# First norm without its gain and bias on the rows, idle transposes at the start, last norm by halves, in a one-core encoder layer

## The chip, the cores and the metric

The kernel runs on one core of a Trainium2 chip. The metric is the time of the whole program on the device in microseconds (us); lower is better. The engines are TensorE (PE; its weight loads are listed apart as PEld), VectorE (DVE), ScalarE (ACT), GpSimd (POOL) and SyncE (SP), which issues most of the DMAs.

## The reference

One post-norm encoder layer over 512 tokens of width 1024, in float32. The parts that the change touches are the first layer norm, the norm after the attention (its input), and the last norm.

```python
def layer_norm(x, g, b):
    xf = x.astype(jnp.float32)
    mu = jnp.mean(xf, axis=-1, keepdims=True)
    var = jnp.mean(jnp.square(xf - mu), axis=-1, keepdims=True)
    y = (xf - mu) * lax.rsqrt(var + LN_EPS)
    return (y * g.astype(jnp.float32) + b.astype(jnp.float32)).astype(x.dtype)
...
    h = layer_norm(x, emb_ln_g, emb_ln_b)
    for i in range(DEPTH):
        z = h @ w_in[i]
        ...
        mix = jnp.concatenate([a_na, a_mla], axis=-1) @ w_o[i]
        h = layer_norm(DN_ALPHA * h + mix, ln1_g[i], ln1_b[i])
        ffn = peer_ffn(h, peer_w_q[i], peer_sub_keys[i], peer_u[i], peer_v[i])
        gate = jax.nn.sigmoid(h @ ple_gate_w[i] + ple_gate_b[i])
        ple = gate * (p[i] @ ple_w[i])
        h = layer_norm(DN_ALPHA * h + ffn + ple, ln2_g[i], ln2_b[i])
    return h
```

`a_na` is a neighbourhood attention, `a_mla` a latent attention, and `peer_ffn` looks up 128 of 16384 experts for each token.

## The kernel before

The 512 tokens are four chunks of 128 rows. `h[0]` to `h[3]` hold the rows of the residual, one token on each partition, 1024 values along it. The matmuls need the transposed activations, `hTh` and `hTl`: every float32 operand is kept as a rounded part (`...h`, "high") and the rest (`...l`, "low"), and a product is three matmuls (`mm3`, lines 93 to 95). `split` (lines 78 and 79) makes the two parts: ScalarE rounds, then VectorE subtracts. So each piece of weight passes through ScalarE and VectorE before PE can use it. A weight is loaded into a buffer `raw`, of which there are three; a fourth load waits until the first has been split.

The first stage (lines 242 to 261) goes over the chunks. For each chunk `layer_norm` takes mean and variance with `bn_stats` and `bn_aggr`, a square root on ScalarE, a reciprocal and a refinement step on VectorE (four operations on one column each), and then two passes over the rows: subtract the mean and multiply by the gain (line 131), multiply by the reciprocal deviation and add the bias (line 134). Gain and bias lie in `eg` and `eb`, broadcast over all partitions by a DMA each (`row_bcast`, line 138). `transpose_to` turns the rows in eight PE transposes in two groups of four, each group into one PSUM tile, and splits each group. Then 24 matmuls against a 1024 x 512 piece of `w_in`, held as `aTh` and `aTl`, make the chunk's values, which ScalarE copies to `v_na` (line 261). The piece of `w_in` comes in four quarters of 256 rows, loaded and split after the first chunk's transposes (lines 252 to 256).

The attention heads follow (lines 287 to 556), first the eight heads of the neighbourhood attention, then those of the latent attention, each as 32 units of scores, softmax and product; the order on PE is written out by hand there, scores two units ahead. Then `w_o` is applied, the residual `h` times `ALPHA` is added (lines 572 and 585), and `layer_norm` is called with `ln1`'s gain and bias (`lg`, `lb`) and with row sums that the addition has gathered; in this form it takes the variance from a squaring pass on ScalarE (line 121). Routing, the expert stage and the last norm (lines 1013 to 1024) come after. In the expert stage the order of VectorE is written by hand; chunk 0 is fed by gathered expert rows, and chunks 1 to 3 by matmuls into the PSUM tiles `acc`. The last norm adds `acc` to the rows in two halves with their sums, calls `layer_norm` and stores each chunk with one DMA.

Where no order is written by hand, a planner at build time makes the order of every engine and queue: it goes through the program with its own estimates of times, and gives an engine that is free the earliest instruction in program order that is ready. The order is then fixed, and on the chip each engine executes it in turn. The memory of a pool that opens later is that of pools closed before; a load into it waits for their last readers.

Of the kernel before, what the change touches and what calls it, by code (L numbers as in the profile page):

```python
# [18 lines left out]
D = 1024  # L19
# [26 lines left out]
FEED_NA = 2.75  # L46
FEED_LAT = 1.0
# [7 lines left out]
def tile_encoder_layer(ctx: ExitStack, tc: tile.TileContext, A: dict, out: bass.AP):  # L55
# [48 lines left out]
    def layer_norm(r, g, b, sums=None, scr=None):  # L104

        ve = small.tile([128, 1], F32, name="ln_ve")
        mu = small.tile([128, 2], F32, name="ln_mu")
        if sums is None:
            st = small.tile([128, 2, 6], F32, name="ln_st")
            for i in range(2):  # L110
                nc.vector.bn_stats(st[:, i, :], r[:, i * 512:(i + 1) * 512])
            nc.vector.bn_aggr(mu, st)
            nc.vector.tensor_scalar(ve, mu[:, 1:2], EPS, None, op0=OP.add)
            neg = None
        else:
            neg = mu[:, 1:2]
            nc.vector.tensor_tensor(neg, sums[:, 0:1], sums[:, 1:2], op=OP.add)
            nc.vector.tensor_scalar(neg, neg, -1.0 / D, None, op0=OP.mult)
            sq = wst.tile([128, D], F32, name="raw", bufs=3) if scr is None else scr
            ss = small.tile([128, 1], F32, name="ln_ss")  # L120
            nc.scalar.activation(sq, r, AF.Square, bias=neg, accum_out=ss)
            nc.vector.tensor_scalar(ve, ss, 1.0 / D, EPS, op0=OP.mult, op1=OP.add)
# [7 lines left out]
        if neg is None:  # L130
            nc.vector.scalar_tensor_tensor(r, r, mu[:, 0:1], g, op0=OP.subtract, op1=OP.mult)
        else:
            nc.vector.scalar_tensor_tensor(r, r, neg, g, op0=OP.add, op1=OP.mult)
# [17 lines left out]
    def ps_tile(name, bufs=2):  # L151
        return ps6.tile([128, 512], F32, name=name, bufs=bufs)
# [17 lines left out]
    def transpose_to(dst_h, dst_l, src, c):  # L170

        for g in range(2):
            ps = ps_tile("tr")
            for i in range(4):
                d = 4 * g + i
                nc.tensor.transpose(ps[:, i * 128:(i + 1) * 128], src[:, d * 128:(d + 1) * 128], ident)
            v = ps.rearrange("p (a b) -> p a b", b=128)
# [64 lines left out]
    with tc.tile_pool(name="ln0", bufs=1) as ln0:  # L242
        nc.sync.dma_start(h[0], A["x"][0:128, :])
        eg = row_bcast(ln0, A["emb_ln_g"], "eg")
        eb = row_bcast(ln0, A["emb_ln_b"], "eb")
        for c in range(1, 4):
            nc.sync.dma_start(h[c], A["x"][c * 128:(c + 1) * 128, :])
# [864 lines left out]
```

## Time and profile before

| | us |
|---|---|
| three timed runs | 1636.96, 1638.03, 1643.42 |
| median | 1638.03 |
| the profiled execution | 1644.48 |
| its span on the core | 1642.7 |

The profile is of one execution. Its page gives busy time by engine, the chain of work that ended last, and the costliest groups of instructions. The timeline lists single instructions: start, duration, engine, line, operation, output and inputs, and in brackets how long the engine had been idle before it and what ended that. "x3" after a row means that neighbouring rows are merged, and then the duration is that from the first start to the last end. A table by stage gives the busy time of the engines in stretches of the span. Durations of neighbouring instructions on an engine overlap by some hundredths to tenths of a us, so that the step from one start to the next is shorter than the duration.

### The profile page before, as it was taken

What the parts mean: (1) busy time and instruction counts of PE and PEld (TensorE: products, weight loads), DVE (VectorE), ACT (ScalarE), POOL (GpSimd) and SP (SyncE); (2) the same over time, 40 slices, a digit from 0 to 9 for tenths busy, and PEclk for the clock granted to TensorE, in tenths of its full rate; (3) what the DMA queues carried; (4) which work ended last, traced back from release to release, by engine and by line L of the source; (5) the groups of instructions that cost most, each with busy time, mean ns of one, the idle gap of its engine ahead of it and who ended that gap; (6) DMA issues with size and microseconds to landing.
All of it is one profiled execution on the core that took longest, in us unless ns stands there. A gap on an engine that the chain in (4) does not pass through costs nothing.

```text
span 1642.7 us, 23609 instructions
## 1 busy us (share of the span) xinstructions
PE 1564.1 (95%) x8195; PEld 1309.7 (80%) x8195; DVE 1328.0 (81%) x2959; ACT 671.3 (41%) x1190; POOL 553.3 (34%) x407
## 2 busy tenths in 40 slices
PE   6999899999999999996899999999999999999997
PEld 4788677888777767784788888888898888888885
DVE  7366794699999999995778888878888888877776
ACT  3356684433324626682333333333343333333343
POOL 1013100000114453200455555555455565543200
PEclk9999999999999999998899999999999999999999
DMA  7242340332469988756899999999999999987763
GB/s 223 61 127 75 86 124 14 119 90 78 118 219 318 373 320 301 288 226 233 309 340 323 359 325 350 361 323 336 354 324 334 358 327 350 344 291 257 260 237 110
DMA packets 190583, 409.13 MB, mean 249 GB/s; under 512 B 14592, under 2 KB 100992, under 8 KB 187392
## 3 DMA queue, kind: packets, MB, share of 16 engines
q1 hardware_dynamic: 141696, 234.06, 41.9%
q0 software_dynamic: 48768, 173.56, 29.3%
q8 instruction: 65, 1.06, 0.3%
q14 instruction: 54, 0.44, 0.1%
HBM read 372.64 MB, written 31.98 MB: 246 GB/s over the span
## 4 chain that ended last, share of the span: by engine, by line
PE 40%; DMA 22%; issue 15%; DVE 14%; POOL 7%; ACT 2%; SPq 1%; DVEq 0%; POOLq 0%; ACTq 0%
DMA gat<-in_u_rows_dram,i_sel 11%; DMA gat<-in_v_rows_dram,i_sel 8%; PE hp L631 4%; PE acc L93 4%; PE acc L95 4%; PE acc L94 4%; POOL gat L925 3%; PE tr L804 3%; PE pj L93 3%; PE mm L93 3%; PE pj L94 3%; PE pj L95 3%; PE mm L94 3%; PE mm L95 3%; POOL gat L936 3%
## 5 line engine op out<-in xcount | busy, mean ns | idle before, releaser
L93 PE MATMUL acc<-v_hi,a_hi 128*128 128x512 f32 x756 | 297.6, 394 | 14.2 <-ACT a_hi L78 14.2
L95 PE MATMUL acc<-v_hi,a_lo 128*128 128x512 f32 x756 | 296.8, 393 | 0.0
L94 PE MATMUL acc<-v_lo,a_hi 128*128 128x512 f32 x756 | 294.9, 390 | 0.0
L925 POOL DMA_INDIRECT gat<-in_u_rows_dram,i_sel x128 | 203.2, 1588 | 260.2 <-DVE scr L927 147.8
L936 POOL DMA_INDIRECT gat<-in_v_rows_dram,i_sel x128 | 210.6, 1646 | 202.7 <-DVE base L938 172.6
L78 ACT CAST a_hi<-gt 128x384 fp32r<-128x384 f32 x126 | 64.9, 515 | 478.7 <-DVE gt L995 476.5
L95 PE MATMUL hp<-hTh,wlo 128*128 128x320 f32 x672 | 211.2, 314 | 17.9 <-DVE wlo L79 17.5
L93 PE MATMUL hp<-hTh,whi 128*128 128x320 f32 x672 | 208.7, 311 | 1.0 <-ACT ge L633 1.0
L94 PE MATMUL hp<-hTl,whi 128*128 128x320 f32 x672 | 208.2, 310 | 0.0
L631 PE MATMUL hp<-whole,raw 128*128 128x320 f32 x704 | 200.3, 433 | 0.0
L78 ACT CAST whi<-raw 128x1024 fp32r<-128x1024 f32 (+3 forms) x137 | 138.4, 1010 | 131.2 <-PE mm L94 53.1
L79 DVE TENSOR_TENSOR wlo<-raw,whi 128x1024 fp32r<-128x1024 f32 (+3 forms) x137 | 159.8, 1167 | 37.7 <-ACT whi L78 37.3
L79 DVE TENSOR_TENSOR v_lo<-v_raw,v_hi 128x1024 fp32r<-128x1024 f32 x126 | 153.7, 1220 | 39.4 <-DMA v_raw<-in_v_rows_dram 19.6
L927 DVE SCALAR_TENSOR_TENSOR scr<-gat,h 128x1024 f32<-128x1024 f32 x128 | 156.5, 1223 | 35.5 <-DMA gat<-in_u_rows_dram,i_sel 33.7
L938 DVE SCALAR_TENSOR_TENSOR base<-gat,hdot,base 128x1024 f32<-128x1024 f32 x128 | 164.1, 1282 | 21.6 <-DMA gat<-in_v_rows_dram,i_sel 20.1
L93 PEld LDWEIGHTS acc<-v_hi,a_hi 128*128 128x128 f32 x756 | 142.3, 188 | 41.9 <-ACT a_hi L78 15.4
L95 PEld LDWEIGHTS acc<-v_hi,a_lo 128*128 128x128 f32 x756 | 142.3, 188 | 33.7 <-DVE a_lo L79 1.4
L631 PEld LDWEIGHTS hp<-whole,raw 128*128 128x128 f32 x704 | 128.9, 190 | 45.6
L94 PEld LDWEIGHTS acc<-v_lo,a_hi 128*128 128x128 f32 x756 | 142.5, 188 | 27.6
L78 ACT CAST v_hi<-v_raw 128x1024 fp32r<-128x1024 f32 x126 | 131.9, 1047 | 54.6 <-PE acc L95 33.4
L95 PEld LDWEIGHTS hp<-hTh,wlo 128*128 128x128 f32 x672 | 127.3, 189 | 26.0 <-DVE wlo L79 25.9
L79 DVE TENSOR_TENSOR a_lo<-gt,a_hi 128x384 fp32r<-128x384 f32 x126 | 70.4, 559 | 80.4 <-ACT a_hi L78 79.1
(343 smaller groups left out, 2863.9 us busy)
## 6 DMA issues: line engine op xcount, KB each, us to landing
raw<-in_uT_dram SPq DMA_DIRECT2D x128, 512.0 KB
v_raw<-in_v_rows_dram SPq DMA_DIRECT2D x128, 512.0 KB
g_dram<-g_st SPq DMA_DIRECT2D x24, 1024.0 KB
gt<-g_dram SPq DMA_DIRECT2D x16, 1536.0 KB
raw<-in_w_in_dram SPq DMA_DIRECT2D x17, 512.0 KB
raw<-in_w_q_dram SPq DMA_DIRECT2D x16, 512.0 KB
na_b<-in_na_bias_dram POOLq DMA_DIRECT2D x32, 128.0 KB
raw<-in_w_o_dram SPq DMA_DIRECT2D x8, 512.0 KB
```

Of the source, the lines that this page charges most:

```text
L78: nc.scalar.copy(hi, src)
L79: nc.vector.tensor_tensor(lo, src, r32(hi), op=OP.subtract)
L93: nc.tensor.matmul(ps, a[0], b[0], start=start, stop=False)
L94: nc.tensor.matmul(ps, a[0], b[1], start=False, stop=False)
L95: nc.tensor.matmul(ps, a[1], b[0], start=False, stop=stop)
L631: nc.tensor.matmul(ps[:, :N_U], u[:, k], whole[:, k, :], start=(k == 0), stop=(k == 7))
L804: nc.tensor.matmul(ps[:, i * 128:(i + 1) * 128], oj[:, 4 * r + i, :], oi[:, 4 * r + i, :], start=True, stop=True)
L925: nc.gpsimd.indirect_dma_start(out=u[:], out_offset=None, in_=u_rows, in_offset=bass.IndirectOffsetOnAxis(ap=i_sel[:, c, k:k + 1], axis=0))
L927: nc.vector.scalar_tensor_tensor(scr, u, 1.0, h[c], op0=OP.mult, op1=OP.mult, accum_out=hdot[:, c, k:k + 1])
L936: nc.gpsimd.indirect_dma_start(out=u[:], out_offset=None, in_=v_rows, in_offset=bass.IndirectOffsetOnAxis(ap=i_sel[:, c, k:k + 1], axis=0))
L938: nc.vector.scalar_tensor_tensor(base[c], u, hdot[:, c, k:k + 1], base[c], op0=OP.mult, op1=OP.add)
```

## The change

The first norm's rows are now only centred and scaled, in one pass with two column operands. Gain and bias of this norm are loaded as columns, `e_gain` and `e_bias` (128 partitions x 8), each by a DMA of single floats, and are applied by ScalarE on the way out of the transposes, eight activations for each chunk into new tiles `tr_y`, which are then split as before. The rows in `h` lack them therefore; they are put in before the first use of the residual, after the heads: two row broadcasts into the buffers of `lg` and `lb`, and a multiplication and an addition for each chunk. `ln1`'s gain and bias are loaded into the same buffers afterwards.

The loads at the start are in another order: `x` of chunk 0, gain, bias, then quarters of the weight and chunks of `x` in turn; the fourth quarter, and `h[3]` behind it, come in the loop. 24 transposes of the identity matrix into a PSUM tile that nothing reads stand ahead of the first norm.

The last norm takes mean and variance with `bn_stats` for all chunks, adds `acc` without row sums, and does each of its two passes and the store in halves of 512 columns. `layer_norm` with sums stays for `ln1`.

```diff
+WARM = 24
...
-    def layer_norm(r, g, b, sums=None, scr=None):
...
+    def inv_dev(ve):
...
+    def row_stats(r):
+
+        st = small.tile([128, 2, 6], F32, name="ln_st")
+        for i in range(2):
+            nc.vector.bn_stats(st[:, i, :], r[:, i * 512:(i + 1) * 512])
+        mu = small.tile([128, 2], F32, name="ln_mu")
+        nc.vector.bn_aggr(mu, st)
+        ve = small.tile([128, 1], F32, name="ln_ve")
+        nc.vector.tensor_scalar(ve, mu[:, 1:2], EPS, None, op0=OP.add)
+        return mu[:, 0:1], inv_dev(ve)
+
+    def layer_norm(r, g, b, sums):
...
-    def transpose_to(dst_h, dst_l, src, c):
+    def transpose_to(dst_h, dst_l, src, c, affine=None):
...
+            if affine is not None:
+                gain, bias, pool = affine
+                y = pool.tile([128, 512], F32, name="tr_y", bufs=3)
+                for i in range(4):
+                    d = 4 * g + i
+                    nc.scalar.activation(y[:, i * 128:(i + 1) * 128], ps[:, i * 128:(i + 1) * 128], AF.Identity,
+                                         scale=gain[:, d:d + 1], bias=bias[:, d:d + 1])
+                ps = y
...
-        eg = row_bcast(ln0, A["emb_ln_g"], "eg")
-        eb = row_bcast(ln0, A["emb_ln_b"], "eb")
-        for c in range(1, 4):
-            nc.sync.dma_start(h[c], A["x"][c * 128:(c + 1) * 128, :])
+        gain = ln0.tile([128, 8], F32, name="e_gain")
+        bias = ln0.tile([128, 8], F32, name="e_bias")
+        for t, src in ((gain, A["emb_ln_g"]), (bias, A["emb_ln_b"])):
+            nc.sync.dma_start(t, bass.AP(tensor=src.tensor, offset=src.offset, ap=[[1, 128], [128, 8]]))
+        raws = []
+        for kk in range(3):
+            raws.append(wst.tile([128, 2, 512], F32, name="raw", bufs=3))
+            nc.sync.dma_start(raws[kk], A["w_in"][kk * 256:(kk + 1) * 256, 1024:1536].rearrange(
+                "(k p) n -> p k n", p=128))
+            if kk < 2:
+                nc.sync.dma_start(h[1 + kk], A["x"][(1 + kk) * 128:(2 + kk) * 128, :])
+        warm = ps_tile("mm")
+        for i in range(WARM):
+            nc.tensor.transpose(warm[:, 0:128], ident, ident)
         for c in range(4):
-            layer_norm(h[c], eg, eb)
-            transpose_to(hTh, hTl, h[c], c)
+            mu, y = row_stats(h[c])
+            nc.vector.tensor_scalar(h[c], h[c], mu, y, op0=OP.subtract, op1=OP.mult)
+            transpose_to(hTh, hTl, h[c], c, (gain, bias, ln0))
             if c == 0:
                 for kk in range(4):
-                    raw = wst.tile([128, 2, 512], F32, name="raw", bufs=3)
-                    nc.sync.dma_start(raw, A["w_in"][kk * 256:(kk + 1) * 256, 1024:1536].rearrange(
-                        "(k p) n -> p k n", p=128))
-                    split(aTh[:, 2 * kk:2 * kk + 2], aTl[:, 2 * kk:2 * kk + 2], raw)
+                    if kk == 3:
+                        raws.append(wst.tile([128, 2, 512], F32, name="raw", bufs=3))
+                        nc.sync.dma_start(raws[kk], A["w_in"][kk * 256:(kk + 1) * 256, 1024:1536].rearrange(
+                            "(k p) n -> p k n", p=128))
+                        nc.sync.dma_start(h[3], A["x"][384:512, :])
+                    split(aTh[:, 2 * kk:2 * kk + 2], aTl[:, 2 * kk:2 * kk + 2], raws[kk])
...
     lnp = p3.enter_context(tc.tile_pool(name="lnp", bufs=1))
+
+    eg = row_bcast(lnp, A["emb_ln_g"], "lg")
+    eb = row_bcast(lnp, A["emb_ln_b"], "lb")
+    for c in range(4):
+        nc.vector.tensor_tensor(h[c], h[c], eg, op=OP.mult)
+        nc.vector.tensor_tensor(h[c], h[c], eb, op=OP.add)
     lg = row_bcast(lnp, A["ln1_g"], "lg")
     lb = row_bcast(lnp, A["ln1_b"], "lb")
...
     for c in range(4):
-        fsum = None
+        r = base[c]
+        halves = [slice(hf * 512, (hf + 1) * 512) for hf in range(2)]
         if c >= NGC:
-            fsum = small.tile([128, 2], F32, name="fsum", bufs=2)
-            for hf in range(2):
-                hs = slice(hf * 512, (hf + 1) * 512)
-                nc.vector.scalar_tensor_tensor(base[c][:, hs], base[c][:, hs], 1.0, acc[c - NGC][hf], op0=OP.mult,
-                                               op1=OP.add, accum_out=fsum[:, hf:hf + 1])
-        layer_norm(base[c], lg, lb, fsum, scr)
-        nc.sync.dma_start(out[c * 128:(c + 1) * 128, :], base[c])
+            for hf, hs in enumerate(halves):
+                nc.vector.tensor_tensor(r[:, hs], r[:, hs], acc[c - NGC][hf], op=OP.add)
+        mu, y = row_stats(r)
+        for hs in halves:
+            nc.vector.scalar_tensor_tensor(r[:, hs], r[:, hs], mu, lg[:, hs], op0=OP.subtract, op1=OP.mult)
+            nc.vector.scalar_tensor_tensor(r[:, hs], r[:, hs], y, lb[:, hs], op0=OP.mult, op1=OP.add)
+            nc.sync.dma_start(out[c * 128:(c + 1) * 128, hs], r[:, hs])
```

`inv_dev` holds the square root, reciprocal and refinement that `layer_norm` had inline.

More of the change, by code (lines that the diff above doesn't have):

```diff
@@ L102, in rsqrt_refine @@
         nc.vector.tensor_tensor(y, t, y0, op=OP.mult)
-    def layer_norm(r, g, b, sums=None, scr=None):
[L106 to L122, printed above, removed]
+    def inv_dev(ve):
         sd = small.tile([128, 1], F32, name="ln_sd")
```

16 lines of the change are left out of this document (12 added, 4 removed).

## The prediction

> **What bounds the kernel now.** I read the page first (span, engines), then the table by stage, then the timelines of the first 47 us and of the last 20, because the change touches these two ends and one place between.
>
> ```profile
> span 1642.7 us, 23609 instructions
> PE 1564.1 (95%) x8195; PEld 1309.7 (80%) x8195; DVE 1328.0 (81%) x2959; ACT 671.3 (41%) x1190; POOL 553.3 (34%) x407
> 0.00:16.00 16.00, 2.38 (x9) 1.85 (x9) 10.50 (x25) 4.29 (x7) 0.71 (x6) 1.00 0.90 313
> 16.00:33.00 17.00, 15.60 (x65) 11.97 (x65) 16.39 (x33) 7.68 (x13) 0.52 (x1) 1.00 0.67 184
> ```
>
> (After the stretch and its length: busy time of PE, PEld, DVE, ACT, POOL, then granted clock, DMA share, GB/s.) TensorE (PE) is busy for 95% of the span; what it loses, it loses mostly at the ends. In the first 16 us it works 2.38 us, and in the next 17 VectorE (DVE) is busy for 16.39. The head is set by arriving data, then by VectorE:
>
> ```profile
> 4.09 1.29 DVE L111 BATCH_NORM_STATS2 ln_st<-h 128x6 f32<-128x512 f32 x2 [3.04 <-DMA h<-in_x_dram]
> 7.19 1.28 DVE L131 SCALAR_TENSOR_TENSOR h<-h,ln_mu,eg 128x1024 f32<-128x1024 f32 x1 [1.39 <-DMA eg<-in_emb_ln_g_dram]
> 10.78 1.94 PE L176 MATMUL tr<-ident,h 128*128 128x128 f32 x8 [10.78 <-DVE h L134]
> 17.42 0.38 SPq L254 DMA_DIRECT2D raw<-in_w_in_dram  x1
> 21.00 1.05 ACT L78 CAST aTh<-raw 128x1024 fp32r<-128x1024 f32 x1 [2.03 <-DMA raw<-in_w_in_dram]
> 23.09 1.22 DVE L79 TENSOR_TENSOR aTl<-raw,aTh 128x1024 fp32r<-128x1024 f32 x1
> 25.84 0.59 ACT L261 COPY v_na<-pj 128x512 f32<-128x512 f32 x1
> 31.29 0.40 PE L95 MATMUL pj<-aTh,hTl 128*128 128x512 f32 x1
> 32.86 0.50 PE L93 MATMUL pj<-aTh,hTh 128*128 128x512 f32 x1 [0.29 <-ACT hTh L78]
> 46.30 0.59 ACT L261 COPY v_na<-pj 128x512 f32<-128x512 f32 x1 [5.72 <-PE pj L95]
> ```
>
> The first norm waits 1.39 us for the broadcast gain; but what ends chunk 0 (its copy to `v_na` at 25.84) is the fourth quarter of the weight: issued at 17.42 when a `raw` buffer came free, cast at 21.00, split by VectorE only at 23.09. From its arrival to the copy it is 25.84 - 21.00 = 4.8 us. After that each chunk is PE's work plus a gap (31.29 + 0.23 to 32.86: 1.3 us) of transposes, cast and split. The fourth copy, at 46.30, is the end of the stage and the point by which I judge the head; PE is dense behind it.
>
> **The head, step by step.** Out go two 512 KB broadcasts and, on VectorE, two 1.28 us passes a chunk; one subtract-and-multiply pass comes in.
>
> ```profile
> L189 DVE TENSOR_SCALAR p_exp<-p_exp,rs 128x512 f32<-128x512 f32 x32 | 15.4, 482 | 0.5
> L189 DVE TENSOR_SCALAR p_exp<-p_exp,rs 128x256 f32<-128x256 f32 x32 | 11.7, 364 | 0.9
> DMA packets 313, 0.08 MB, mean 198 GB/s; under 512 B 256, under 2 KB 282, under 8 KB 313
> q1 hardware_dynamic: 313, 0.08, 88.7%
> 10.70:13.00 2.30, 1.94 (x8) 1.57 (x8) 2.30 (x5) 0.83 (x2) 0.00 (x0) 1.00 1.04 403
> ```
>
> 256 columns more cost 0.118 us, so 1024 cost 0.482 + 2 x 0.118 = 0.72, and VectorE is relieved of 4 x (2.56 - 0.72) = 7.4 us. The gain and bias now come as 2 x 1024 descriptors of 4 bytes. The two DMA rows are the stretch 20.2 to 20.6 us, in which `gq` and `gk` land (256 packets of 8 and 12 bytes): 0.4 us x 16 engines x 88.7% = 5.7 us for all 313, at most 22 ns a small one; less 57 larger ones, some 10. So 2048 take 1.3 to 2.8 us. At the 403 GB/s of the last row 512 KB take 1.3 us. First quarter of the weight: 4.1 (x there) + 1.3 to 2.8 + 1.3 = 6.7 to 8.2. Its cast and split (1.05 + 1.22, and 0 to 1 behind other VectorE work) free the buffer at 9 to 11.5; the fourth quarter needs 21.0 - 17.4 = 3.6 us from issue, and 4.8 to the copy: 17.4 to 19.9. I take 19.3, nearer the late end because VectorE has three chunks' statistics waiting too: 6.5 us earlier than 25.84.
>
> Against this stand eight scale-and-bias activations a chunk on ScalarE (ACT):
>
> ```profile
> L783 ACT ACTIVATE ne<-tr x3: 278/278/279, 512.3 to 691.8; 128x128 f32<-128x128 f32 x3
> L295 ACT ACTIVATE p_t<-pj,gk x2: 679/682/685, 52.4 to 57.8; 128x512 f32<-128x512 f32 x2
> 32.21 1.09 ACT L78 CAST hTh<-tr 128x512 fp32r<-128x512 f32 x2
> 23.61 1.04 PE L176 MATMUL tr<-ident,h 128*128 128x128 f32 x8
> ```
>
> 0.28 for 128 columns out of PSUM, and 0.09 more with an operand as scale (0.68 against 0.59 for the copy): 0.37; back to back 0.1 less (two casts in 1.09). Four stand between transposes and the cast: 1.1 to 1.5 us on each gap, I take 1.3. Chunk 1's transposes ran at 23.61, inside chunk 0's wait, and can again; so two gaps grow, three at worst: 2.2 to 4.5, taken 2.6. Head: -6.5 + 2.6 = **-3.9**, from -6.2 (17.4 and 2.2) to -1.4 (19.9 and 4.5). `h[3]` now queues on SP behind the fourth quarter's wait for a buffer, as do the next weights; chunk 3 needs it past 30 us, so this is hidden.
>
> The 24 idle transposes run while PE has nothing to do (free up to 10.78), and chunk 0's pace is set by the weight, so I put them at 0; at a slow step they gain at most what follows:
>
> ```profile
> 19.95 0.43 PE pj L93
> 23.07 0.23 PE pj L94
> ```
>
> Ten matmuls at 0.43 instead of 0.23 are 2 us, which show only if nothing else holds chunk 0. [...]
>
> **The late gain and bias.** Eight VectorE passes of 1.22 us (the price of L79 above, same shape) = 9.8 us, behind two more 512 KB loads.
>
> ```profile
> L138 SPq DMA_DIRECT2D lg<-in_ln_g_dram x1: 341/341/341, 181.0 to 181.0; - x1
> 181.00:200.00 19.00, 16.33 (x107) 12.77 (x105) 15.46 (x37) 12.69 (x27) 0.00 (x0) 1.00 0.28 83
> 200.00:220.00 20.00, 19.44 (x143) 15.63 (x144) 18.30 (x41) 17.50 (x35) 2.94 (x6) 1.00 0.44 139
> 220.00:240.00 20.00, 18.95 (x141) 14.40 (x140) 17.91 (x43) 15.96 (x34) 0.98 (x2) 1.00 0.41 117
> 240.00:260.00 20.00, 19.99 (x160) 15.43 (x158) 14.55 (x40) 14.28 (x30) 0.00 (x0) 1.00 0.09 27
> 260.00:276.20 16.20, 16.20 (x83) 12.96 (x82) 4.37 (x4) 4.35 (x5) 0.00 (x0) 1.00 0.10 33
> 276.23 0.69 DVE L572 SCALAR_TENSOR_TENSOR h<-h,mm 128x512 f32<-128x512 f32 x1 [1.08 <-PE mm L95]
> ```
>
> The buffers open at 181 and the results are needed at 276.23. VectorE is free for 79 - 66.2 = 12.8 us up to 260 and 11.8 more after it, so there is room; but a pass of 1.22 us in a gap of the softmax work holds up the row maximum behind it, and PE waits for that chain. Bounds: 0, if they fall behind 260, and 4.9, half of each pass exposed. I take a quarter of 4.9, **+1.2**, as the heads are issued two units ahead. ln1's own loads now wait on SP for these passes, with the `w_o`, `pT` and `ple_w` loads behind them; they need be there only about 260, so 0 while the passes run before 240.
>
> **The tail.**
>
> ```profile
> 5.41 0.21 DVE L112 BATCH_NORM_AGGREGATE ln_mu<-ln_st 128x2 f32<-128x12 f32 x1
> 1623.06 0.69 DVE L1021 SCALAR_TENSOR_TENSOR h<-h,acc 128x512 f32<-128x512 f32 x1 [0.69 <-PE acc L95]
> 1624.28 0.08 DVE L1021 DVE_READ_ACCUMULATOR h<-h,acc 128x1 f32 x1
> 1624.40 0.16 DVE L117 TENSOR_TENSOR ln_mu<-fsum 128x1 f32<-128x1 f32 x1
> 1637.47 1.28 DVE L134 SCALAR_TENSOR_TENSOR h<-h,ln_y,gat 128x1024 f32<-128x1024 f32 x1
> 1623.00:1632.60 9.60, 9.60 (x44) 7.75 (x42) 8.03 (x26) 2.90 (x6) 0.00 (x0) 1.00 0.12 47
> 1632.60:1638.75 6.15, 0.17 (x1) 0.00 (x0) 5.77 (x19) 1.45 (x3) 0.00 (x0) 0.78 0.25 100
> ```
>
> From 1623.06 to the last pass's end, 1638.75, VectorE works 13.8 of 15.7 us. The squares leave ScalarE (busy 1.45 us in the last stretch, squares and root) and become two `bn_stats` and an aggregate a chunk on VectorE: 6 x 0.64 (two took 1.29 at 4.09) + 3 x 0.21 = 4.5 more; less 6 accumulator reads of 0.08 and two small sums a chunk of some 0.1 each, overlapped, 1.1 in all. Halving the passes adds little, say 0.1. That makes 17.3 us: the end moves by +1.6 if all idle time is filled, by +3.5 if none is; taken +2.2. The last store is 256 KB instead of 512: at 403 GB/s 0.65 less. Tail **+1.6** (1.0 to 2.9). A gain is excluded, since VectorE already waits for PE at 1623.06.
>
> **The sum** is -3.9 + 1.2 + 1.6 = -1.1 us. The profiled execution took 1644.48 (span 1642.7 and 1.8 around it): 1643.4 after. The three times shown have the median 1638.03, 6.4 lower; against it 1636.9. Bounds: -6.2 + 0 + 1.0 = -5.2 and -1.4 + 4.9 + 2.9 = +6.4, 1632.8 to 1644.4.
>
> **Rivals.** B, the head gives more: the planner fills chunk 0's wait for the fourth quarter with chunk 1's matmuls and chunk 2's transposes. For: PE would idle there some 2.3 us (18 of 24 matmuls done, at 0.23 each, from about 10.5 to 14.7, against 17) and the norms are shorter. Against: before, it put only chunk 1's transposes in. -6.2 - 2.3 (idle filled) - 1.1 (one gap that does not grow) + 0 + 1.0 = -8.6: 1629.4. C, slower: the late passes make VectorE the bound of the latent heads. It decides if they all land between 181 and 240, where VectorE works 51.7 of 59 us; 9.8 more are past the full 59, and each pass shows whole: -1.4 + 9.8 + 1.6 = +10.0: 1648. For: the loads are ready at 181 and the planner fills any free slot. Against: they come last in program order. D, the head doesn't do what it says: 4-byte descriptors cost as much as the average packet of SP's queue:
>
> ```profile
> q1 hardware_dynamic: 141696, 234.06, 41.9%
> ```
>
> 0.419 x 16 x 1642.7 / 141696 = 78 ns, so 2048 take 9.9 us. The first quarter comes at 15.3, chunk 0 ends near 27: +1.2 instead of -6.5, in all +6.6: 1644.6. Against it: the 22 ns bound.
>
> **Chances.** Forecast 0.47, B 0.22, C 0.22, D 0.09. About 0.5% (8.2 us) is what a measurement of this kernel can tell from no change. B lies at that edge; I count somewhat more than half of it as faster: 0.14. C is slower: 0.22. The rest is 0.64. The range reaches past the middle of B and to that of C: 1628 to 1648; the likeliest case alone has 1632.8 to 1644.4.
>
> **What would show it.** Right: the first `v_na` copy near 19.3 and the fourth near 42.4; scale-and-bias activations of 0.28 to 0.37; the eight late passes spread over 181 to 276 with PE's busy share there unchanged; VectorE ending some 8 us after the last matmul instead of 6. Wrong: weights that arrive after 9 us, matmuls waiting for the row maximum in the latent heads, or a changed order in the expert stage, which I hold to be the same.

## The result and the profile after

| | before | changed |
|---|---|---|
| median of 6 timed runs, us | 1640.33 | 1657.12 |
| lowest to highest | 1636.96 to 1647.56 | 1653.52 to 1661.83 |
| span of the profiled execution | 1642.7 | 1656.2 |

The ratio is 1.0093, with a 95% interval of 1.0067 to 1.0119: the change makes the kernel slower by some 15 us. Five points along the two traces, and the end of the span, tell where the 13.5 us between the two spans come from (start times, us):

| point | before | changed | later by |
|---|---|---|---|
| first copy to `v_na` | 25.84 | 26.03 | 0.2 |
| fourth copy to `v_na` | 46.30 | 53.31 | 7.0 |
| first row maximum of the latent heads | 178.22 | 185.87 | 7.6 |
| first residual add after `w_o` | 276.23 | 289.59 | 13.4 |
| first add of an accumulator in the last norm | 1623.06 | 1635.50 | 12.4 |
| end of the span | 1642.7 | 1656.2 | 13.5 |

So the head costs 7 us, the latent heads 5.7, the tail 1.1, and the long stages between give or take a us. (Lines of the changed kernel: splits 79 and 80, transposes 182, scale-and-bias 188, the pass over the rows 274, matmuls 94 to 96.)

**The head.** Rows of the timeline of the changed kernel:

```profile
7.92 1.09 PE L182 MATMUL tr<-ident,h 128*128 128x128 f32 x8 [1.47 <-DVE h L274]
...
7.93 1.05 ACT L79 CAST aTh<-raw 128x1024 fp32r<-128x1024 f32 x1 [1.87 <-DMA raw<-in_w_in_dram]
...
10.53 1.04 ACT L79 CAST aTh<-raw 128x1024 fp32r<-128x1024 f32 x1 [1.56 <-DMA raw<-in_w_in_dram]
...
13.15 1.04 ACT L79 CAST aTh<-raw 128x1024 fp32r<-128x1024 f32 x1 [1.57 <-DMA raw<-in_w_in_dram]
...
14.10 1.85 ACT L188 ACTIVATE tr_y<-tr,e_bias,e_gain 128x128 f32<-128x128 f32 x5
...
15.82 0.63 ACT L79 CAST hTh<-tr_y 128x512 fp32r<-128x512 f32 x1
...
16.50 0.79 PE L94 MATMUL pj<-aTh,hTh 128*128 128x512 f32 x1 [7.49 <-ACT hTh L79]
...
17.23 0.69 DVE L120 BATCH_NORM_STATS2 ln_st<-h 128x6 f32<-128x512 f32 x1 [1.49 <-DMA h<-in_x_dram]
...
22.23 2.25 DVE L274 TENSOR_SCALAR h<-h,ln_mu,ln_y 128x1024 f32<-128x1024 f32 x3
...
26.03 0.58 ACT L288 COPY v_na<-pj 128x512 f32<-128x512 f32 x1 [2.74 <-PE pj L96]
...
28.93 0.50 PE L94 MATMUL pj<-aTh,hTh 128*128 128x512 f32 x1 [0.20 <-ACT hTh L79]
...
45.59 0.50 PE L94 MATMUL pj<-aTh,hTh 128*128 128x512 f32 x1 [2.06 <-ACT hTh L79]
...
53.31 0.59 ACT L288 COPY v_na<-pj 128x512 f32<-128x512 f32 x1 [6.06 <-PE pj L96]
```

The first half of what was wanted is there: `x` is normed early, and chunk 0's eight transposes begin at 7.92 instead of 10.78. Then nothing happens on PE for 7.5 us. ScalarE executes its order in turn, and in this order three weight casts stand ahead of chunk 0's activations. Each of them waits for its own transfer (1.87, 1.56 and 1.57 us, the brackets), so the transposed rows that lie ready in PSUM at 9.0 are touched only at 14.10. Five activations and a cast later the first matmul starts, at 16.50; before, it started at 15.56. The three later chunks' rows are finished on VectorE only from 22.23 on, behind all the weight's splits, and in PE's order chunk 1's transposes stand behind chunk 0's matmuls. (Up to 17.23 VectorE also stood 1.49 us for the rows of the last chunk, whose load is now behind the fourth quarter's, with the low part of chunk 0's first four blocks behind them; PE waited 0.84 us for that.) From the end of chunk 0's matmuls (25.83) to chunk 1's first one at 28.93 are 3.1 us, and the gap before chunk 3 (42.49 to 45.59) is the same: transposes, four activations, cast. The gap before chunk 2 is 0.4, as half of its transposes found a place in the first gap. The table by stage gives the clock (columns after the stretch: PE, PEld, DVE, ACT, POOL, granted clock, DMA share, GB/s):

```profile
9.10:16.50 7.40, 0.00 (x0) 0.00 (x0) 6.39 (x11) 4.39 (x9) 0.00 (x0) 0.52 0.90 333
20.00:23.00 3.00, 3.00 (x9) 2.31 (x8) 3.00 (x19) 1.81 (x2) 0.00 (x0) 0.50 0.65 172
29.00:33.50 4.50, 4.50 (x12) 3.28 (x13) 1.99 (x3) 3.46 (x9) 0.00 (x0) 0.62 0.21 41
46.00:50.50 4.50, 4.50 (x14) 3.43 (x13) 0.96 (x2) 1.22 (x3) 2.22 (x5) 0.62 0.27 61
```

In its idle us up to 16.50 PE falls to half its clock (0.52 granted from 9.10 to 16.50), and chunk 0's first twelve matmuls, up to 23.00, go at it (0.50 from 20.00 to 23.00). The fourth quarter of the weight, asked for at 10.26 and split by 20.7, no longer holds up the chunk. The clock falls again behind both long gaps (0.62 granted over 4.5 us each time): 12 and 14 matmuls in 4.5 us instead of 20, at 0.43 a step instead of 0.23. Gaps of 6.6 us in all against 2.9 before, and two times some eight matmuls with 0.2 lost on each, make 0.2 + 3.7 + 3.2 = 7.1.

**The latent heads.** Rows of VectorE and PE in the changed kernel:

```profile
185.87 0.69 DVE L535 TENSOR_REDUCE mx<-mm 128x1 f32<-128x512 f32 x1 [2.20 <-PE mm L96]
...
195.23 1.22 DVE L591 TENSOR_TENSOR h<-h,lg 128x1024 f32<-128x1024 f32 x1
...
209.90 0.67 DVE L495 TENSOR_TENSOR p_exp<-pj,cosT 128x512 f32<-128x512 f32 x1
...
210.62 0.67 PE L94 MATMUL pj<-cqh,whi 128*128 128x512 f32 x1 [3.82 <-DVE p_exp L495]
...
216.24 1.22 DVE L592 TENSOR_TENSOR h<-h,lb 128x1024 f32<-128x1024 f32 x1
...
220.86 0.63 PE L208 MATMUL tr<-ident,p_exp 128*128 128x128 f32 x4 [0.94 <-DVE nmx L198]
...
237.62 0.50 PE L94 MATMUL hp<-hTh 128*128 128x512 f32 x1
...
289.59 0.69 DVE L605 SCALAR_TENSOR_TENSOR h<-h,mm 128x512 f32<-128x512 f32 x1 [1.08 <-PE mm L96]
```

Before:

```profile
178.22 0.69 DVE L508 TENSOR_REDUCE mx<-mm 128x1 f32<-128x512 f32 x1 [2.47 <-PE mm L95]
...
200.56 0.53 PE L93 MATMUL pj<-cqh,whi 128*128 128x512 f32 x1 [2.02 <-DVE p_exp L468]
...
224.35 0.50 PE L93 MATMUL hp<-hTh 128*128 128x512 f32 x1
```

All eight late passes run between 195.23 and 217.4, in the middle of the softmax work. The rotary product (`p_exp`, line 495 now, 468 before) comes late, with five of them ahead of it, and PE stands 3.82 us for it instead of 2.02. Behind this wait PE steps at half clock for some three us (0.53 granted from 210.60 to 214.00), which it did not before (1.00 from 200.50 to 204.00). At 220.86 it stands 0.94 us for a late row maximum (`nmx`). The matmul in the last PE row of each listing is the same one: it starts 51.8 us behind the first row maximum now and 46.1 before. So 5.6 us are lost by there, and from the first row maximum to the first residual add it is 103.7 us instead of 98.0. (Up to there PE has its score and projection matmuls in the same order in both kernels; behind it the orders differ.)

**The tail.**

```profile
1635.50 1.28 DVE L1053 TENSOR_TENSOR h<-h,acc 128x512 f32<-128x512 f32 x2 [0.69 <-PE acc L96]
...
1651.64 1.41 DVE L1057 SCALAR_TENSOR_TENSOR h<-h,ln_y,gat 128x512 f32<-128x512 f32 x2
```

From the first add to the end of VectorE it is 17.55 us (1651.64 + 1.41 - 1635.50) instead of 15.7, and the smaller last store gives 0.8 of it back: 20.7 from the first add to the span's end, against 19.64.

### The profile page after: what moved, and what is told of

Its sections match the earlier page's. It is cut to its first block, busy times and chain, and to the rows that moved or that the text cites. A ratio compares the mean times of both kernels' runs of the same rounds, so it can differ in the third digit from the quotient of the medians.

```text
span 1656.2 us, 23704 instructions
## 1 busy us (share of the span) xinstructions
PE 1572.6 (95%) x8219; PEld 1317.0 (80%) x8219; DVE 1333.7 (81%) x2968; ACT 678.4 (41%) x1216; POOL 547.8 (33%) x407
## 4 chain that ended last, share of the span: by engine, by line
PE 38%; DMA 18%; DVE 17%; issue 16%; POOL 9%; ACT 1%; DVEq 0%; SPq 0%; POOLq 0%; ACTq 0%
DMA gat<-in_u_rows_dram,i_sel 8%; DMA gat<-in_v_rows_dram,i_sel 7%; POOL gat L958 5%; PE acc L94 4%; PE acc L96 4%; PE acc L95 4%; DVE oh_j L832 3%; POOL gat L969 3%; PE pj L94 3%; PE pj L96 3%; PE pj L95 3%; PE mm L94 3%; PE mm L96 3%; PE mm L95 3%; PE hp L664 2%
## 5 line engine op out<-in xcount | busy, mean ns | idle before, releaser
L969 POOL DMA_INDIRECT gat<-in_v_rows_dram,i_sel x128 | 206.7, 1615 | 205.6 <-DVE base L971 176.9
```

Source lines behind the costliest of these rows:

```text
L969: nc.gpsimd.indirect_dma_start(out=u[:], out_offset=None, in_=v_rows, in_offset=bass.IndirectOffsetOnAxis(ap=i_sel[:, c, k:k + 1], axis=0))
```

## The experiments

All kernels are compared at the same points. The columns are: first and fourth copy to `v_na`; from the first row maximum of the latent heads to the first residual add; from there to the first add of an accumulator; from there to the end of the span.

| kernel | 1st copy | 4th copy | latent heads | routing, experts | tail |
|---|---|---|---|---|---|
| before | 25.84 | 46.30 | 98.0 | 1346.8 | 19.6 |
| changed | 26.03 | 53.31 | 103.7 | 1345.9 | 20.7 |
| e1 no late passes | 25.21 | 49.37 | 98.5 | 1350.1 | 20.9 |
| e2 no idle transposes | 22.44 | 50.53 | 102.0 | 1347.3 | 20.7 |
| e3 no scale and bias | 23.73 | 45.54 | 103.1 | 1350.9 | 20.7 |
| e4 tail alone | 26.82 | 46.94 | 98.4 | 1347.0 | 20.9 |
| e5 ScalarE's order | 23.30 | 53.92 | 104.9 | 1351.2 | 20.7 |
| e6 head by hand | 32.88 | 59.10 | 104.5 | 1348.4 | 20.7 |
| e7 late on GpSimd | 25.85 | 50.03 | 108.6 | 1355.5 | 20.8 |
| e8 late after softmax | 26.02 | 51.75 | 104.5 | 1351.5 | 20.7 |
| e9 late by halves | 25.74 | 52.98 | 99.5 | 1350.2 | 20.7 |
| e10 head held | 23.25 | 40.78 | 104.4 | 1346.1 | 20.8 |
| e11 combined | 23.27 | 40.85 | 98.6 | 1343.9 | 20.1 |
| e12 the same, no idle transposes | 23.19 | 40.75 | 100.5 | 1355.6 | 20.1 |
| e13 combined again | 23.14 | 40.71 | 98.2 | 1347.4 | 20.0 |
| e14 no idle transposes again | 23.34 | 40.91 | 97.7 | 1348.2 | 20.1 |

The fifth column is the yardstick for single executions: its source is nowhere touched, and two executions of one kernel (e12 and e14) differ there by 7.4 us. A total of one execution therefore says little here; totals are used only where nine or more timed executions stand behind them. The points are steadier, but not fixed: in the latent heads e12 and e14 differ by 2.8 us too (VectorE stands 1.65 us for PE at the row maximum of 200.41 in e12, and not at all at the same one in e14, 197.56), so a difference of some 3 us in that column is not read alone. With the late passes in their place on VectorE the column has 102.0 to 104.9 (six kernels); without them, or with them by halves, 97.7 to 100.5 (eight).

### One part taken out

**e1**, the eight late passes and their two loads left out:

```diff
-    eg = row_bcast(lnp, A["emb_ln_g"], "lg")
-    eb = row_bcast(lnp, A["emb_ln_b"], "lb")
-    for c in range(4):
-        nc.vector.tensor_tensor(h[c], h[c], eg, op=OP.mult)
-        nc.vector.tensor_tensor(h[c], h[c], eb, op=OP.add)
```

> Leaves out the late gain and bias of the residual: the two 512 KB loads and the eight VectorE passes behind them. Theory (the passes delay the row maxima and the rope chain of the latent heads): from the first latent row maximum to the first residual add the run takes about 98 us as before the change (98.0), not 103.7; the first residual add starts near 283.5, the total falls by about 6 against the changed kernel. Rival (the stretch is longer because of another order of loads or of the planner's instructions that the head's change brings): that stretch stays above 102 us and the total moves by less than 2.

The latent heads went back to 98.5: the theory's figure, and the rival fell. The ratio to the kernel before is 1.0051 (1.0028 to 1.0075), down from 1.0093. In the order made at build time some projection matmuls stand elsewhere on PE when the passes are there than when they are not, but only from 54 us behind the first row maximum on. At 51.8 us the changed kernel is already 5.5 us behind e1, and at the residual add 5.2: the other order costs nothing that shows. One thing came unasked: the fourth copy at 49.37 instead of 53.31, though up to the latent heads PE, ScalarE and VectorE have the same order in both kernels. Stretches behind the two long gaps in this execution, which end at 28.11 and 43.21:

```profile
29.00:33.50 4.50, 4.50 (x20) 3.64 (x21) 1.39 (x2) 2.65 (x7) 0.00 (x0) 1.00 0.20 36
44.00:46.00 2.00, 2.00 (x10) 1.64 (x10) 0.69 (x1) 0.84 (x2) 0.29 (x1) 1.00 0.00 0
```

Here the clock stayed at 1.00 after both gaps: 20 matmuls in 4.5 us and 10 in 2, where the changed kernel's execution had 12 and 14 in 4.5 us. So some 3.2 us of the 7.0 in the head are the clock's, and differ between executions of one order: e7, whose order there is also the same, lost none; e8 lost one gap's worth and e9 both, with the head unchanged in the source.

**e2**, without the idle transposes:

```diff
-WARM = 24
+WARM = 0
```

> No idle transposes (24 to 0). Theory (TensorE stands still from 9.0 to 16.5 whatever came before, so the clock they raised is lost again): chunk 0's eight transposes take 1.9 us instead of 1.09, the first matmul stays at 16.5 within 1 us and steps 0.43, the fourth copy stays at 53.3 within 1 us. Rival (the transposes are what brought the clock and some of the order): the fourth copy moves by more than 2 us.

```profile
8.05 1.94 PE L182 MATMUL tr<-ident,h 128*128 128x128 f32 x8 [8.05 <-DVE h L274]
...
11.70 1.85 ACT L188 ACTIVATE tr_y<-tr,e_bias,e_gain 128x128 f32<-128x128 f32 x5
...
14.11 0.80 PE L94 MATMUL pj<-aTh,hTh 128*128 128x512 f32 x1 [4.12 <-ACT hTh L79]
```

The transposes take 1.94 again, as expected, and the rest of the expectation missed: the first matmul came 2.4 us earlier, the fourth copy 2.8. Without the 24 transposes the order made at build time has the activations ahead of the third cast (11.70 instead of 14.10), presumably because PE counts as free sooner in it. So the idle transposes seem to cost the changed kernel something, through ScalarE's order.

**e3**, the rows split straight from the transposes, so that all projections lack the first norm's gain and bias:

```diff
-            transpose_to(hTh, hTl, h[c], c, (gain, bias, ln0))
+            transpose_to(hTh, hTl, h[c], c)
```

> The transposed rows are cast and split directly, so the first norm's gain and bias are left out of the projections. Theory (the scale-and-bias activations between transposes and cast are what lengthens the gaps and drops the clock in them): the gaps between the chunks fall from 6.6 us in all to about 3, the matmuls after them step 0.23, the fourth copy comes near 45 (43 to 47). Rival 1 (ScalarE's fixed order alone, three weight casts ahead of chunk 0's, is the loss): only the 1.9 us of activations of chunk 0 are won, the fourth copy stays near 51. Rival 2 (VectorE, whose statistics of chunks 1 to 3 stand behind the fourth quarter's split, sets the gaps): the gaps stay above 5 us, fourth copy near 49.

```profile
23.53 1.04 PE L182 MATMUL tr<-ident,h 128*128 128x128 f32 x8
...
24.85 0.50 PE L94 MATMUL pj<-aTh,hTh 128*128 128x512 f32 x1 [0.29 <-ACT hTh L79]
...
45.54 0.59 ACT L288 COPY v_na<-pj 128x512 f32<-128x512 f32 x1 [5.72 <-PE pj L96]
```

The theory held: 1.3 us from the end of chunk 0 (23.53, where the transposes begin) to chunk 1's first matmul instead of 3.1, the same at the next gaps, no matmuls at 0.43 a step behind them (1.00 granted from 23.00 on, in stretches of 2 and 3 us up to 52.00), fourth copy at 45.54. Ratio 1.0047 (1.0023 to 1.0072). With this and e1 the two large parts are separated: each is about 0.4% of the time.

**e4**, the kernel before with the new last norm alone (`row_stats` and the halves, as in the change):

```diff
-        layer_norm(base[c], lg, lb, fsum, scr)
...
+        mu, y = row_stats(r)
+        for hs in halves:
+            nc.vector.scalar_tensor_tensor(r[:, hs], r[:, hs], mu, lg[:, hs], op0=OP.subtract, op1=OP.mult)
+            nc.vector.scalar_tensor_tensor(r[:, hs], r[:, hs], y, lb[:, hs], op0=OP.mult, op1=OP.add)
```

> The kernel before with the new last norm and nothing else of the change. Theory: everything up to the first add of an accumulator (1623.1) is as before, from there to the span's end it takes about 20.7 instead of 19.6 us: total +1.1, within what can be told from no change. Rival (part of the 12 to 13 us of the whole change comes from a new order that the last norm brings to the planner): the first add moves by more than 2 us.

Tail 20.9 against 19.6: +1.2, and nothing moved ahead of it beyond 1.7 us. Ratio 1.0009 (0.9993 to 1.0026), no difference that can be told.

### Towards an order that pays

**e5**, ScalarE's order in the head by hand:

```diff
+        with tc.manual_schedule(engines={nc.scalar.engine}):
+            norm(0)
+            tr = [turned(h[0], g) for g in range(2)]
+            w_split(0)
+            placed(tr[0], hTh, hTl, 0, 0, aff)
...
+            w_split(1)
+            placed(tr[1], hTh, hTl, 0, 1, aff)
+            w_split(2)
+            w_split(3)
```

(`turned` are the four transposes of a group, `placed` its activations and split, `w_split` a weight quarter's split.)

> Only ScalarE's order in the head is written by hand: first weight cast, first half of chunk 0 (activations, cast), second weight cast, second half, third and fourth weight cast, the roots of chunks 1 to 3, then chunk by chunk. Theory (three weight casts that wait for their transfers stand ahead of chunk 0's activations): the first matmul comes at 11 to 12 instead of 16.5, chunk 0's copy at 18 to 21 instead of 26.0; the gaps between chunks stay at about 3 us each, so the fourth copy at 45 to 50 instead of 53.3. Rival (VectorE or the weight's transfers set chunk 0, ScalarE's order does not): the first copy stays above 23.

```profile
11.49 0.80 PE L94 MATMUL pj<-aTh,hTh 128*128 128x512 f32 x1 [2.29 <-ACT hTh L79]
...
19.21 2.31 DVE L80 TENSOR_TENSOR aTl<-raw,aTh 128x1024 fp32r<-128x1024 f32 x2
...
23.30 0.58 ACT L312 COPY v_na<-pj 128x512 f32<-128x512 f32 x1 [1.36 <-PE pj L96]
```

Half right. The first matmul came at 11.49, five us earlier: the three casts were what held it. But chunk 0's copy stayed at 23.30, on the rival's side, because the third and fourth quarter's split sits on VectorE at 19.21, behind statistics that the planner had put first; and the fourth copy came no earlier (53.92). ScalarE's order alone is not the head's whole loss; VectorE's is the next.

**e6**, the three engines by hand, the next chunk's transposes ahead of a chunk's matmuls:

```diff
+        with tc.manual_schedule(engines={nc.tensor.engine, nc.scalar.engine, nc.vector.engine}):
...
+            w_split(2)
+            norm(1)
+            w_split(3)
+            ps = product(0)
...
+            for c in range(1, 4):
+                tr = [turned(h[c + 1], g) for g in range(2)] if c < 3 else []
+                ps = product(c)
+                for g in range(len(tr)):
+                    placed(tr[g], hTh, hTl, c + 1, g, aff)
+                nc.scalar.copy(v_na[:, c, :], ps)
```

> TensorE, ScalarE and VectorE in the head are written by hand: as in the run before, and the transposes, activations and casts of the next chunk come ahead of a chunk's matmuls or beside them. Theory (the loss in the head is order alone, the operations themselves have room): first copy 18 to 21, only one gap of 1 to 3 us (behind chunk 0), fourth copy at 38 to 42, that is 4 to 8 before the kernel before (46.3) and 11 to 15 before the changed one. Rival (the added activations are work that does not fit beside the matmuls): fourth copy above 45.

```profile
11.32 0.79 PE L94 MATMUL pj<-aTh,hTh 128*128 128x512 f32 x1 [2.18 <-ACT hTh L79]
...
20.20 1.04 ACT L79 CAST whi<-raw 128x1024 fp32r<-128x1024 f32 x1 [4.99 <-DMA raw<-in_w_in_dram]
...
21.25 1.03 ACT L79 CAST aTh<-raw 128x1024 fp32r<-128x1024 f32 x1
...
37.53 1.94 PE L181 MATMUL tr<-ident,h 128*128 128x128 f32 x8 [7.94 <-DVE h L287]
```

A miss, and the most instructive one: fourth copy at 59.10. An order by hand keeps its own instructions in sequence, but the planner still puts others between them. It put a cast of the next stage's weight (`whi`) in at 20.20, where ScalarE stood 4.99 us for that transfer, ahead of chunk 1's root and of the fourth quarter's cast at 21.25. The mechanism of the changed kernel again, one instruction further on. The order by hand has a second loss of the same kind, and a larger one: chunk 2's transposes stand ahead of chunk 1's matmuls on PE, chunk 2's rows come late on VectorE, and PE stood 7.94 us for them (37.53) while chunk 1's operands had been ready since about 33.7.

**e10** repairs this. The next stage's splits are queued behind the head's last split, the fourth quarter gets a tile of its own instead of waiting for a `raw`, all loads are issued at the start, and statistics, transposes and activations of a chunk lie inside the chunk ahead:

```diff
+            product(0, ps[0], range(6))
+            tr = [turned(h[1], g) for g in range(2)]
+            product(0, ps[0], range(6, 8))
...
+                product(c, ps[c], range(4))
+                if c < 3:
+                    tr = [turned(h[c + 1], g) for g in range(2)]
+                product(c, ps[c], range(4, 8))
...
+        with tc.issue_after(head_end[0].ins), tc.issue_after(head_end[1].ins):
+            for part in (latent_k(0, lat_k), latent_k(1, lat_k), na_proj(0)):
```

> The head by hand again, with three differences: the next stage's weight casts are queued behind the head on ScalarE and VectorE (in the run before ScalarE stood 5 us at such a cast whose transfer was late), the fourth quarter of the weight has a tile of its own, and each chunk's statistics and transposes come inside the chunk ahead. Theory (operations that wait for transfers, ahead of others in a fixed order, are the whole loss in the head): first matmul at 11 to 12, first copy at 20 to 23.5, no gap over 1 us, fourth copy at 39 to 42 (before 46.3, change 53.3). Rival (the added activations or VectorE do not fit): fourth copy above 45.

```profile
11.42 0.79 PE L97 MATMUL pj<-aTh,hTh 128*128 128x512 f32 x1 [1.39 <-ACT hTh L81]
...
21.25 0.50 PE L97 MATMUL pj<-aTh,hTh 128*128 128x512 f32 x1 [0.41 <-ACT hTh L81]
...
28.18 0.50 PE L97 MATMUL pj<-aTh,hTh 128*128 128x512 f32 x1
...
36.58 2.00 ACT L81 CAST whi<-raw 128x1024 fp32r<-128x1024 f32 x2
...
40.78 0.59 ACT L320 COPY v_na<-pj 128x512 f32<-128x512 f32 x1 [2.21 <-PE pj L99]
```

The theory held: first matmul at 11.42, chunk 1's at 21.25 with 0.41 us of waiting, chunk 2's without any, fourth copy at 40.78, which is 5.5 before the kernel before and 12.5 before the changed one. The same eight activations a chunk leave no gap here. (The first copy, 23.25, is no measure of chunk 0 here: its last matmul begins at 20.43, and ScalarE makes the copy behind chunk 1's activations.) Which of the three differences to e6 does how much was not taken apart.

### The late passes elsewhere

**e7**, the passes on GpSimd:

```diff
-        nc.vector.tensor_tensor(h[c], h[c], eg, op=OP.mult)
-        nc.vector.tensor_tensor(h[c], h[c], eb, op=OP.add)
+        nc.gpsimd.tensor_tensor(h[c], h[c], eg, op=OP.mult)
+        nc.gpsimd.tensor_tensor(h[c], h[c], eb, op=OP.add)
```

> The eight late passes of gain and bias run on GpSimd instead of VectorE; loads and their order as in the change. Theory (VectorE's time is what the passes take from the latent heads): from the first latent row maximum to the first residual add 98 to 99.5 us instead of 103.7. Rival 1 (the loads and the w_o transfers behind them do it): it stays above 102. Rival 2 (GpSimd's passes slow VectorE's down as they run): 100 to 103, with VectorE's own groups longer.

VectorE's groups from 191 to 211, while they run, and one of the passes' own groups (least, median and longest ns):

```profile
L203 DVE TENSOR_SCALAR p_exp<-p_exp,rs 128x512 f32<-128x512 f32 x6 | 7.9, 1323 | 0.1
L535 DVE TENSOR_REDUCE mx<-mm 128x1 f32<-128x512 f32 x5 | 3.3, 684 | 0.1
```

```profile
L591 POOL TENSOR_TENSOR h<-h,lg x4: 2399/2515/2579, 191.7 to 203.9; 128x1024 f32<-128x1024 f32 x4
```

The theory fell: 108.6, longer than rival 2 asked, and rival 2's sign is there, VectorE's groups are longer. A pass takes 2.5 us on GpSimd against 1.22, and VectorE's scaling of the probabilities, from SBUF to SBUF, takes 1323 ns instead of 481 meanwhile, while its row maxima out of PSUM stay at 684. A split of 128 x 256 with both inputs in SBUF took 2.44 us beside GpSimd and 0.41 in the kernel before. Why these are slower and the row maxima are not, no row shows. The loads of rival 1 are not excluded by this run alone; e1 left out loads and passes together, and e9, which keeps the two loads ahead of `w_o`, has 99.5.

**e8**, the passes queued on VectorE behind the last softmax operation, `ln1`'s loads last:

```diff
+    with tc.issue_after(soft_end[-1].ins):
...
-    lg = row_bcast(lnp, A["ln1_g"], "lg")
-    lb = row_bcast(lnp, A["ln1_b"], "lb")
...
+    lg = row_bcast(lnp, A["ln1_g"], "lg")
+    lb = row_bcast(lnp, A["ln1_b"], "lb")
```

> The eight late passes are queued on VectorE behind the last softmax operation, and ln1's loads are asked for last. Theory (a pass costs nothing where VectorE has no softmax to do): 9.8 us of passes lie in the 16 us up to the first residual add, the stretch from the first latent row maximum to it is 98 to 99.5 us. Rival (the passes only come later on the path): the stretch is shorter than 103.7, but the first residual add waits for VectorE instead of TensorE, or the adds behind it come later by more than 2 us.

```profile
265.59 2.35 DVE L594 TENSOR_TENSOR h<-h,lg 128x1024 f32<-128x1024 f32 x2
...
275.66 2.35 DVE L80 TENSOR_TENSOR wlo<-raw,whi 128x1024 fp32r<-128x1024 f32 x2
...
276.93 0.79 PE L95 MATMUL mm<-wlo,aTh 128*128 128x512 f32 x1 [2.99 <-DVE wlo L80]
```

A miss too: 104.5. The softmax work took 79.2 us from the first to the last row maximum, as before (78.7), but the passes then ran as one block from 265.59 on, with `w_o`'s last two splits behind them, and PE stood 2.99 us for those at 276.93, with a lower clock after it (0.90 granted from 260 to 280). VectorE had the room, but not ahead of the splits.

**e9**, by halves behind those splits, the second halves behind the first residual adds:

```diff
+    def late(lo, hi):
+        for t, op in ((eg, OP.mult), (eb, OP.add)):
+            for c in range(4):
+                nc.vector.tensor_tensor(h[c][:, lo:hi], h[c][:, lo:hi], t[:, lo:hi], op=op)
...
+    with tc.issue_after(split_end[1].ins):
+        late(0, 512)
...
+    with tc.issue_after(added.ins):
+        late(512, 1024)
```

> The late gain and bias go by halves: columns 0 to 511 of the four chunks (eight passes of 0.69) queued on VectorE behind the last split of w_o, columns 512 to 1023 behind the four first residual adds; ln1's loads are asked for after them. Theory (a late pass costs what it delays on VectorE: nothing if neither the softmax chain nor a weight's split waits behind it): from the first latent row maximum to the first residual add 98 to 99.5 us (before 98.0, change 103.7, whole passes behind the softmax 104.5). Rival (any place on VectorE costs about half of the 9.8 us): 102 or more, or the later residual adds come 3 us or more later after the first than before (8.0 us from the first to the adds behind w_o's second half).

```profile
278.26 2.49 DVE L596 TENSOR_TENSOR h<-h,lg 128x512 f32<-128x512 f32 x4
...
284.87 0.69 DVE L610 SCALAR_TENSOR_TENSOR h<-h,mm 128x512 f32<-128x512 f32 x1 [0.58 <-PE mm L99]
...
293.48 0.68 DVE L627 SCALAR_TENSOR_TENSOR h<-h,pj 128x512 f32<-128x512 f32 x1
```

The theory held: 99.5, and 8.6 us from the first residual add to the first add behind it (284.87 to 293.48) instead of 8.0. The gain and bias that cost 5.7 us between the softmax units cost 1.5 and then 0.6 here, which is within what executions of one kernel differ by.

### The parts put together

**e11** is e9 and e10 in one with the last norm of the kernel before, **e12** the same without idle transposes; **e13** and **e14** time both side by side.

> The two kernels above in one, with the last norm of the kernel before. Theory: head -5 to -7, latent heads 0 to +1.5, tail 0 against the kernel before: a ratio of 0.996 to 0.998. Rival (what is gained in the head is lost again behind it, as the stages there keep their own pace): a ratio within 0.999 to 1.003, with the first latent row maximum no earlier than 177.

> The combined kernel without its 24 idle transposes, in the same order written by hand. Theory (the idle transposes cost or save only through the order that a planner chooses; here ScalarE paces chunk 0): the eight transposes of chunk 0 take about 1.95 us, the first matmul comes within 0.3 us of 11.44 and the fourth copy within 0.5 us of 40.85. Rival (they bring the clock that the first matmuls need): the fourth copy 1 us or more later.

> The combined kernel once more. Theory: a ratio to the kernel before of 0.996 to 1.000, as in its first five rounds (0.9983). Rival (its first result was one chip's luck): above 1.000.

> The combined kernel without the 24 idle transposes once more, beside the run above. Theory (they are worth nothing here; the long expert stage of the one look was a spread of single executions): within 0.1% of the combined kernel, a ratio of 0.996 to 1.000 to the kernel before. Rival (they matter in a way that the head does not show): 0.3% or more above the combined kernel again.

| kernel | median | before, same chip | ratio | 95% interval |
|---|---|---|---|---|
| e11 combined | 1641.88 | 1643.98 | 0.9983 | 0.9967 to 1.0000 |
| e13 combined again | 1638.97 | 1645.35 | 0.9965 | 0.9944 to 0.9985 |
| e14 no idle transposes | 1641.19 | 1645.35 | 0.9978 | 0.9957 to 0.9999 |

The combined kernel is faster than the one before, by some 0.2 to 0.35%, about what the points of e11 and e13 say: head -5.5, latent heads +0.2 to +0.6, tail +0.4 (the tail's source is that of the kernel before; why it is longer is open). e12's head agrees with its expectation (transposes 1.94, fourth copy 40.75). Its one total, 1651.2, did not come back in e14, so it was the spread of single executions. e14's median lies 0.14% above e13's instead of the 0.1% expected at most, well inside both intervals: idle transposes are worth nothing here that can be told.

## Why the prediction was wrong

The forecast was 1636.9 us, in a range of 1628 to 1648; 1657.12 lies outside it. Between the forecast sum of -1.1 us and the 13.5 of the spans lie 14.6, of which 10.9 in the head and 4.5 in the late passes.

**What bounds the head.** Right that the weight's arrival and VectorE set the head of the kernel before, and that its first copy ends it. The step that failed is the one to 19.3 us: "Its cast and split (1.05 + 1.22, and 0 to 1 behind other VectorE work)". It followed the weight from transfer to split, and the rows from `x` to transposes, but each engine as if it took whatever was ready. In the order made at build time the weight's casts stood ahead of chunk 0's activations, and each waited for its transfer. The fourth quarter was asked for at 10.26, as forecast (9 to 11.5), but no longer ended the chunk: the first matmul came at 16.50 and twelve went at half clock (0.50 granted from 16.50 to 23.00). The term of -6.5 came out as +0.2. e5 shows the order's share of the first matmul (five us), e10 that the time was to be had: its chunk 0 runs from 11.42, chunk 1 follows at 21.25, and the fourth copy comes at 40.78 (forecast 42.4). Rival B did not come either: nothing of chunk 1 fills chunk 0's wait.

**The activations.** Their price was right: four in 1.50 to 1.54, so four add about 1.5 to a gap where 1.3 was taken. The gaps grew from 2.9 to 6.6, by 3.7 instead of 2.6, since the rows of chunk 1, done late, lost their place inside chunk 0. What the sum did not have at all is the clock that falls behind gaps of 3.1 us: 3.2 us in the profiled execution (0.62 granted behind both), 0 in e1 and e7 (1.00).

**Idle transposes at 0.** On PE this was right: behind them chunk 0's transposes took 1.09 us instead of 1.94, and of that nothing was left at the first matmul (0.52 granted from 9.10 to 16.50, 0.43 a step behind it). But the head came 2 to 3 us earlier without them (e2, one execution), most likely through the order made at build time, a path that the prediction did not look at.

**The loads.** Right for the small descriptors: they are cheap, the first quarter was there for the cast at 7.93 (forecast 6.7 to 8.2), and rival D fell. Wrong for `h[3]`, which was put at 0: VectorE waited for it at 17.23, and PE 0.84 us behind.

**The late passes.** The mechanism was named (a pass "in a gap of the softmax work holds up the row maximum behind it"), and rival C had its place, all eight between 181 and 240. The step that failed is the size: a quarter of 4.9 taken, 5.7 measured, above the bound of 4.9 as well. Half of each pass exposed was no upper bound: the late rotary product cost PE 1.8 us more of waiting, and the half clock behind that wait (0.53 granted for 3.4 us) another 1.5, a cost that the sum did not have. Rival C's price for the passes, all 9.8, was too high, yet of the cases it came nearest: its total of +10 stands beside +13.5 between the profiled spans.

**The tail.** Right: +1.6 taken, +1.1 measured (+1.2 alone, e4).

With the measured sizes in its own sum: +7.0 (head) + 0.6 (up to the latent heads) + 5.7 + 1.1 - 0.9 (routing and experts) = 13.5 us of span. What stays open: the 0.6 ahead of the latent heads, and what decides in which executions the clock falls behind a gap.

## What to carry to other kernels

When a change moves an operation onto an engine, write down that engine's whole order around it, and for each instruction ahead of it what it waits for: an instruction whose transfer is late holds up everything behind it, however ready that is (ScalarE stood 1.87, 1.56 and 1.57 us at three casts of the changed kernel, and 4.99 us at one of e6). Where a planner makes the order from its own estimates, added work changes the order of others, so fix the order by hand there, and queue the next stage's work behind it. And a pass that "fits into idle time" is priced by what stands behind it at that place: the same 9.8 us of passes cost 5.7 us between softmax units, 6.5 as a block ahead of two splits, and about 2, no more than the spread, behind them.

## What the runs showed of the hardware

- The clock after a gap differs between executions of one order. Gaps of 3.1 us between matmuls, in which PE did 1.0 to 1.7 us of transposes, were followed by half clock twice in the changed kernel and e9 (0.62 granted from 29.00 to 33.50 and from 46.00 to 50.50), once in e8 (0.64, then 1.00), never in e1 and e7 (1.00). What decides it no run shows. In the latent heads PE's wait of 3.82 us for the rotary product was followed by half clock in the changed kernel (0.53 granted from 210.60 to 214.00), the wait of 2.02 us in the kernel before was not (1.00 from 200.50 to 204.00).
- Behind idle transposes chunk 0's eight transposes were faster in most executions, not in all: they took 1.09 to 1.10 us in eight of the eleven profiles of kernels that have them, and 1.8 to 1.97 in e1, e10 and e13; without them 1.9 every time. The granted clock from 7.00 to 9.10 reads 1.00 in the changed kernel and 0.71 in e1, but 1.00 in e2 without them too, so that it does not show by itself that they raise the clock.
- Beside GpSimd's passes some VectorE instructions took almost three times as long (481 to 1323 ns), and row maxima out of PSUM as long as before (686 and 684).
